# Moving the attention value products later in the output projections, and turning four score blocks on VectorE instead of TensorE

## The chip, the cores and the metric

The kernel runs on one core of one Trainium2 chip. The metric is the device time of one execution in microseconds (us), median over repeated runs; lower is better.

## The reference

One inference step of a two-layer decoder for two groups that share all weights: a prompt of 256 positions and 8 sample sequences of one position each, 264 columns in all. The width is 1024.

- Layer 0: norm, one input projection (q, k, v, bu, bv), block-sparse attention with 8 heads of 64 (half A of the mix) beside a gated mixer on bu and bv (half B), one output projection, residual.
- Layer 1: the same frame with stick-breaking attention (half A) and a pooling mixer (half B).
- Each layer then has a norm and a gated feed-forward part (2816 wide, causal convolution of width 3 on the gate), residual. A last norm ends it.

The output projection multiplies `concat([a, b_out])` by a 1024 x 1024 matrix. All of it is float32. Outputs are the two results, the new keys and values, the normalised bv rows of the samples, and pooling and convolution states.

## The kernel before, in words

**Products.** Activations lie as 8 tiles of 128 rows by 264 columns. Every weight matrix is cut into blocks of 128 x 128; a phase (`in0`, `out0`, `ff0`, `dn0`, and the same for layer 1) is a list of blocks (output tile m, input tile k), made in `_phases` (L62 to L78), and the host packs the weights in this order. A block costs three matmuls, since weight and activation are each split into a high and a low part of the faster float32 form (`wh`, `wl` and `..._h`, `..._l`). Eight blocks make a weight tile; `split` (L312) has ScalarE write `wh` (L322) and VectorE `wl` (L338) some tiles ahead: three as a rule, fewer where the tables `NEAR` and `LOOK` (L306, L307) say so. `split` also calls `raw` (L297), which loads the float32 weights, 1 MB for two tiles, into one of three buffers, up to two loads ahead.

**Order.** `run` (L365) goes through a phase block by block. TensorE runs in program order. A hook `blk(b, f)` calls f after b blocks of the phase, so its TensorE work stands between blocks, and its other instructions are ranked by that place. All transfers made with `late` (L284) go to SyncE's queue (SP) in program order, so that one that waits holds up those behind it. `behind(i, j)` only puts i after j on its engine.

**Output phases.** `out0` and `out1` are 64 blocks each. Before, four output tiles run side by side: first k = 4 to 7 (half B, the tiles `catB`) for m = 0 to 3, then k = 0 and 1 (half A, `catA`) for m = 0 to 3, then k = 2 and 3, tile by tile, then m = 4 to 7 one after the other. Each open output tile holds a PSUM bank: there are four of the pool `mm`, and four of the pool `at` that serve the small products; blocks listed in `spare` (L363) take one of `at`.

**The value products.** After 8 blocks of `out0` stand the sample products `pv` (L556), the value products `s_av` (L986, `pav`, two heads each), and `sm_out` (L1031, `po`), which together write `catA`. For them the score blocks p of each head must be turned, queries by keys to keys by queries:

- The first 256 columns of all heads go by VectorE's 32 x 32 transposes (`Turn.squares`, L605, tiles `turn0a`, `turn0b`), a write to DRAM (`write`, L610) and four reads back with the squares in their places (`read`, L614). The values take the same way (`turnv`, `v_squares`, L973), in eight reads.
- The last 128 columns of each head ("own") go by TensorE: `s_own` (L965) transposes four heads into PSUM, and ScalarE copies them out (`pT_own`). It is called for heads 0 to 3 after block 123 and for heads 4 to 7 after block 140 of `in0`.

Layer 1 turns its own blocks by VectorE's squares and DRAM (`own_squares`, `own_write`, `own_read`, L1290 to L1309). There the value products stand after 11 blocks of `out1`.

**Other work near it.** The gated mixer ends with `gm_gate` (L1106) and `gm_mul` (L1115), which write `catB`; tile 3 of it is made in `out0` after block 1. The residual input X is loaded after block 2 (`late_x`, L1140), and CSTATE, a state of the convolution, ahead of `out0`; `conv_prep` (L642) works on it.

Of the kernel before, what the change touches and what calls it, by code (L numbers as in the profile page):

```python
# [9 lines left out]
F32 = mybir.dt.float32  # L10
# [8 lines left out]
P = 128  # L19
D = 1024  # L20
KD = D // P
SEQ = 256
# [17 lines left out]
MMB = 4  # L40
KQ, MQ = 5, 6
WARM = 15

# [18 lines left out]
def _phases():  # L62
    k8 = list(range(KD))
    in0 = [(n, t) for n in ("bv", "q", "k", "v", "bu") for t in range(4)]
    q0 = [(m, k) for k in range(KQ) for m in in0[:MQ]] + [(m, k) for m in in0[:MQ] for k in range(KQ, KD)]
    in1 = [(n, t) for n in ("u", "q", "k", "v") for t in range(4)]
    m8 = [("o", t) for t in range(8)]
    kb = [4, 5, 6, 7, 0, 1, 2, 3]
    ff = [(n, j) for j in range(NF) for n in ("g", "u")]
    kf = list(range(NF))  # L70
    ph = []
    for l, ins in enumerate((in0, in1)):
        ph.append((f"in{l}", _split_order(ins, k8, 4) if l else q0 + [(m, k) for m in in0[MQ:] for k in k8]))
        ph.append((f"out{l}", [(m, k) for k in kb[:6] for m in m8[:4]] + [(m, k) for m in m8[:4] for k in kb[6:]] + [(m, k) for m in m8[4:] for k in kb]))
        ph.append((f"ff{l}", _split_order(ff, k8, 4)))
        two = [(m, k) for ks in (kf[:-2], kf[-2:]) for m in m8[:2] for k in ks]
        ph.append((f"dn{l}", two + [(m, k) for m in m8[2:] for k in (kf[2:] + kf[:2] if m[1] % 2 else kf)]))
    return ph  # L78
# [130 lines left out]
def tile_decoder_step(ctx: ExitStack, tc: tile.TileContext, a):  # L209
# [32 lines left out]
    def f4(name, shape=(P, 4, T), dt=F32):  # L242
        return up.tile(list(shape), dt, tag="u", name=name)
# [40 lines left out]
    def late(dst, src, queue=nc.sync):  # L284
        return tc.keep_in_program_order(queue.dma_start(dst, src))
# [19 lines left out]

    LOOK = {19: 1, 21: 2, 105: 2, 106: 2, 107: 2, 108: 1, 109: 1, 110: 0, 111: 2}  # L306
    NEAR = (3, 5, 10, 12, 15, 16, 17, 18)  # L307
# [4 lines left out]
    def split(t):  # L312
        if t == 2:
            raw(7)
        for tt in range(len(splits), min(t + (2 if t in NEAR else LOOK.get(t, 3)), NT - 1) + 1):
# [23 lines left out]
            if tt == 109:  # L339
                behind(i, turned["own", 0])  # L340
            if tt == 6:
                behind(i, summed)
# [19 lines left out]

    spare = (4, 5, 48)  # L363

# [204 lines left out]
    def sample_av_of(st, pz, vtiles, gr, name):  # L569
        return lambda: sample_av(st, pz, vtiles, gr, name)  # L570
# [25 lines left out]
    def flat(z):  # L596
        return z.rearrange({4: "p j x y -> p (j x y)", 5: "p j x y z -> p (j x y z)"}[len(z.shape)])

    class Turn:
# [13 lines left out]

        def read(self, parts=1, queue=nc.sync):  # L614
            self.dst = f4(f"{self.name}_turned", self.shape)
            far = self.far.rearrange("(i p) (j e x) -> p j i e x", i=4, j=4, e=parts)
            for j in range(4):
                to = flat(self.dst)[32 * j:32 * j + 32].rearrange("p (e i x) -> p i e x", i=4, e=parts)
                for e in range(parts):
                    late(to[:, :, e], far[:, j, :, e], queue)  # L620

# [342 lines left out]

    def s_own(n):  # L965
        pt = (mmb, at)[n](f"pt0_own{n}")
        for i in range(4):
            pe.transpose(pt[:, i * P:(i + 1) * P], st0.pop(("p", 4 * n + i))[:, SEQ:384], ident)
        if n == 0:
            st0["own"] = f4("pT0_own", (P, 8, P))  # L970
        turned["t", 3 + n] = s.activation(st0["own"][:, 4 * n:4 * n + 4, :], pt.rearrange("p (i q) -> p i q", q=P), AF.Copy)

    def v_squares(ts):  # L973
        if not turnv:
            turnv.append(Turn("turnv", (4, 2, 32, 4)))
        for t in ts:
            turned["vsq", t] = turnv[0].squares(t, v4[:, t, :], turnv[0].src[:, :, t // 2, :, t % 2::2].rearrange("p j b c -> p c j b"))
            behind(turned["vsq", t], turned["p", 7] if t > 1 else turned["v", 3])

    def v_of(c, h):  # L980
        t = h // 2
        return flat(turnv[0].dst).rearrange("p (e f x) -> p e f x", e=2, x=4)[:, t // 2, HD * (h % 2):HD * (h % 2) + HD, 2 * c + t % 2]

    turn0, turnv = [], []

    def s_av(t):  # L986
        if t == 0:
            catA.extend(mv("catA0"))
        pav = at(f"pav0_{t}")
        for h in (2 * t, 2 * t + 1):  # L990
            av(pav, v_of, turn0[h // 4].of(h % 4), st0["own"][:, h, :], h)
        turned["cat", t] = s.activation(catA[0][:, t, :SEQ], pav[:, :SEQ], AF.Copy)
        v.tensor_tensor(catA[1][:, t, :SEQ], pav[:, :SEQ], catA[0][:, t, :SEQ].bitcast(F32), ALU.subtract)
# [131 lines left out]
    def gm_bu(t):  # L1125
        turned["gelu", t] = s.activation(bu4[:, t, :], bu4[:, t, :], AF.Gelu_apprx_tanh)
        if t == 2:
            behind(turned["gelu", t], turned["sgu", 3])

# [10 lines left out]
    def late_x(m):  # L1140
        late(X[:, m:m + 2, :], a["x"].rearrange("p (m t) -> p m t", t=T)[:, m:m + 2, :])

# [31 lines left out]
    blk(143, sm_tr)  # L1174
    blk(156, lambda: late(a["bvn"], st0["bvn"]))
    for t in range(4):
# [4 lines left out]
    for t in range(3):  # L1181
        blk((138, 145, 153)[t], gm_bu, t)
# [12 lines left out]
    for t in range(4):  # L1195
        blk(8, s_av, t)
    blk(8, sm_out)
    blk(44, lnexp)


    late(CSTATE, a["cstate"].rearrange("p (l i j s) -> p l i j s", l=2, i=2, j=NF))
    for l in range(2):
        conv_prep(l)

# [79 lines left out]
    def z_squares(n):  # L1284
        for i in range(4):
            j = turned["w", 2 * n + 1] = turn1[n].squares(i, st1["w", 4 * n + i])
            if n:
                behind(j, turned["v", 0])

    def own_squares(n):  # L1290
        if n == 0:
            st1["own"] = f4("own1_squares", (P, 2, 4, 4, 32))
        for i in range(4):
            j = v.transpose(st1["own"][:, n, :, i, :], st1.pop(("w", 4 * n + i))[:, SEQ:384].rearrange("p (j b) -> p j b", j=4))
# [5 lines left out]
    def own_write(n):  # L1300
        st1["far", n] = drp.tile([P, 512], F32, tag=f"own1_{n}", name=f"own1_far{n}")
        late(st1["far", n], st1["own"][:, n].rearrange("p j i b -> p (j i b)"))

    def own_read(n):
        if n == 0:
            st1["turned"] = f4("own1_turned", (P, 2, 4, 4, 32))
        far = st1["far", n].rearrange("(a p) (j x) -> p j a x", a=4, j=4)
        for j in range(4):
            late(st1["turned"][32 * j:32 * j + 32, n].rearrange("p a i b -> p a (i b)"), far[:, j])  # L1309

    def z_av(t):
        if t == 0:
            catA.extend(mv("catA1"))
        pav = at(f"pav1_{t}")
        for h in (2 * t, 2 * t + 1):
            av(pav, lambda c, h: vt[:, c, h * HD:(h + 1) * HD], turn1[h // 4].of(h % 4), st1["turned"][:, h // 4, :, h % 4, :], h)
        halves(catA[0][:, t, :SEQ], catA[1][:, t, :SEQ], pav[:, :SEQ])
# [96 lines left out]
    blk(103, turn1[0].write)  # L1414
    blk(104, own_write, 0)
    blk(105, raw, 60)
    blk(105, z_squares, 1)
    blk(112, turn1[0].read)
    blk(112, own_read, 0)
    blk(119, lambda: turn1[1].write())  # L1420
# [10 lines left out]
    blk(2, own_squares, 1)  # L1431
    blk(2, own_write, 1)
    blk(2, own_read, 1)
    for t in (2, 3):
# [8 lines left out]
    for n, z in (("k1", k4), ("v1", v4)):  # L1443
        for i in (0, 2):
            blk(12, late, a[n][:, i:i + 2], z[:, i:i + 2])

# [75 lines left out]
```

## Time and profile before

| | |
|---|---|
| median of 3 runs | 576.15 us (576.0 to 576.34) |
| the profiled execution | 576.39 us |
| its span, first to last instruction | 574.6 us |
| TensorE busy | 569.6 us, 99% of the span |
| VectorE, ScalarE, GpSimd busy | 428.4, 341.8, 113.1 us |
| TensorE's share of the chain that ended last | 97% |
| mean granted TensorE clock | 0.999 |

"The chain that ended last" goes back from the last instruction, at each step to what released it or to the instruction before it on its engine. Work on other engines costs time only where it makes something on this chain wait.

### The profile page before, as it was taken

How to read it: one execution, taken by the hardware profiler on the slowest of the kernel's cores; microseconds unless marked ns; L12 is line 12 of the kernel's file. 1: busy time of each engine (PE TensorE's matmuls, PEld its weight loads, DVE VectorE, ACT ScalarE, POOL GpSimd, SP SyncE). 2: the span in 40 equal slices, each digit the busy share in tenths (PEclk: the TensorE clock that was granted, in tenths of full speed). 3: DMA queues.
4: the chain of work that ended last, by engine and by line, in shares of the span. 5: the costliest groups of instructions: out<-in, count | busy, mean ns of one | idle time of the engine just before them, and what ended most of it. 6: DMA issues, size and time to landing. Idle time of an engine off the chain costs nothing.

```text
span 574.6 us, 12309 instructions
## 1 busy us (share of the span) xinstructions
PE 569.6 (99%) x4865; PEld 555.9 (97%) x4865; DVE 428.4 (75%) x766; ACT 341.8 (59%) x606; POOL 113.1 (20%) x111
## 2 busy tenths in 40 slices
PE   9999999999999999999999999999999999999997
PEld 7998979999999999999999897999999999999996
DVE  6999978797777777865659887788777777775541
ACT  7847857765656555654454675667555565665442
POOL 1110113223232232210120011222222323211010
PEclk9999999999999999999999999999999999999999
DMA  8999889454545545795567697845455454555502
GB/s 322 361 386 362 315 266 384 161 211 148 201 165 178 189 159 209 271 407 210 185 233 266 237 332 197 305 155 204 165 168 200 155 211 149 194 208 200 213 1 76
DMA packets 33451, 128.69 MB, mean 224 GB/s; under 512 B 3954, under 2 KB 8946, under 8 KB 22002
## 3 DMA queue, kind: packets, MB, share of 16 engines
q1 hardware_dynamic: 32816, 127.39, 61.4%
q8 instruction: 38, 0.62, 0.4%
q10 hardware_dynamic: 578, 0.52, 0.3%
q14 instruction: 19, 0.16, 0.1%
HBM read 120.80 MB, written 7.10 MB: 223 GB/s over the span
## 4 chain that ended last, share of the span: by engine, by line
PE 97%; issue 2%; DMA 0%; ACT 0%; POOL 0%; DVE 0%; POOLq 0%; ACTq 0%
PE mm L221 90%; PE sc L221 1%; PE pv_l L221 1%; PE pav L221 1%; PE Z L221 1%; PE S L221 1%; DMA xw<-in_xw 0%; PE pf L221 0%; PE pm L221 0%; PE po_l L224 0%; PE vtp_sgu L224 0%; PE vtp_v L224 0%; PE pt_own L224 0%; POOL acc_fin L481 0%; PE ns_n L221 0%
## 5 line engine op out<-in xcount | busy, mean ns | idle before, releaser
L338 DVE TENSOR_TENSOR wl<-raw,wh 128x1024 fp32r<-128x1024 f32 x178 | 219.5, 1237 | 55.2 <-ACT wh L322 54.8
L322 ACT ACTIVATE wh<-raw 128x1024 fp32r<-128x1024 f32 x178 | 187.3, 1055 | 80.1 <-PE mm L221 68.4
L221 PE MATMUL mm<-xg_f_h,wl 128*128 128x264 f32 x704 | 197.5, 280 | 0.0
L221 PE MATMUL mm<-xg_f_h,wh 128*128 128x264 f32 x704 | 196.9, 280 | 0.0
L221 PE MATMUL mm<-xg_f_l,wh 128*128 128x264 f32 x704 | 196.8, 280 | 0.0
L221 PEld LDWEIGHTS mm<-xg_f_l,wh 128*128 128x128 f32 x704 | 131.9, 187 | 0.0
L221 PEld LDWEIGHTS mm<-xg_f_h,wl 128*128 128x128 f32 x704 | 131.8, 187 | 0.0
L221 PEld LDWEIGHTS mm<-xg_f_h,wh 128*128 128x128 f32 x704 | 131.8, 187 | 0.0
L684 POOL TENSOR_TENSOR wk<-wk 128x264 f32<-128x264 f32 x44 | 66.3, 1510 | 193.7 <-DVE wk L683 170.9
L221 PE MATMUL mm<-a_h,wl 128*128 128x264 f32 x330 | 92.6, 281 | 0.0
L221 PE MATMUL mm<-a_h,wh 128*128 128x264 f32 x330 | 92.3, 280 | 0.0
L221 PE MATMUL mm<-a_l,wh 128*128 128x264 f32 x330 | 92.3, 280 | 0.0
L221 PEld LDWEIGHTS mm<-a_l,wh 128*128 128x128 f32 x330 | 61.8, 187 | 0.0
L221 PEld LDWEIGHTS mm<-a_h,wh 128*128 128x128 f32 x330 | 61.8, 187 | 0.0
L221 PEld LDWEIGHTS mm<-a_h,wl 128*128 128x128 f32 x330 | 61.8, 187 | 0.0
L509 ACT ACTIVATE a_h<-wk 128x264 fp32r<-128x264 f32 x42 | 17.8, 423 | 70.2 <-POOL wk L684 70.2
L510 DVE TENSOR_TENSOR a_l<-wk,a_h 128x264 fp32r<-128x264 f32 x42 | 18.4, 438 | 40.0 <-ACT a_h L509 40.0
L221 PE MATMUL mm<-xg_h,wl 128*128 128x264 f32 x160 | 42.4, 288 | 0.0
L221 PE MATMUL mm<-xg_h,wh 128*128 128x264 f32 x160 | 42.1, 284 | 0.2 <-ACT wh L824 0.2
L221 PE MATMUL mm<-xg_l,wh 128*128 128x264 f32 x160 | 41.5, 281 | 0.0
L221 PE MATMUL mm<-xg_n_h,wl 128*128 128x264 f32 x128 | 36.5, 285 | 0.0
L221 PE MATMUL mm<-xg_n_h,wh 128*128 128x264 f32 x128 | 35.8, 280 | 0.0
(291 smaller groups left out, 931.4 us busy)
## 6 DMA issues: line engine op xcount, KB each, us to landing
raw<-in_w SPq DMA_DIRECT2D x89, 1024.0 KB, 4.8
K<-in_kt SPq DMA_DIRECT2D x32, 256.0 KB, 6.9
V<-in_vp SPq DMA_DIRECT2D x32, 256.0 KB, 6.4
raw<-in_w SPq DMA_DIRECT2D x3, 512.0 KB, 6.3
xw<-in_xw SPq DMA_DIRECT2D x3, 388.0 KB, 5.8
X<-in_x SPq DMA_DIRECT2D x4, 264.0 KB, 9.8
out_y<-y SPq DMA_DIRECT2D x3, 256.0 KB, 2.2
out_k<-k SPq DMA_DIRECT2D x1, 528.0 KB, 9.6
```

The source lines that it names most:

```text
L221: return self.keep(nc.tensor.matmul(*x, **k))
L322: i = s.activation(h, src, AF.Copy)
L338: i = turned["wl", tt] = v.tensor_tensor(l, src, h.bitcast(F32), ALU.subtract)
L509: s.activation(h, src, AF.Copy)
L510: return v.tensor_tensor(l, src, h.bitcast(F32), ALU.subtract)
L684: g.tensor_tensor(A, A, C, ALU.mult)
```

## The change

- In `out0` and `out1` five output tiles run side by side; the fifth takes a bank of the pool `at`. Half B now covers 20 blocks.
- Layer 0's value products stand after 16 blocks of `out0` (before 8), those of layer 1 after 14 of `out1` (before 11).
- Layer 0's own blocks of heads 4 to 7 go by VectorE's squares and DRAM, in a class `OwnTurn` that layer 1 now uses too. They are turned in `out0` after block 5, behind `wl` of tile 21, written and read back on SP.
- The values are stored in another order (8 elements between neighbours instead of 4), which takes four reads instead of eight; their last two squares stand behind `wl` of tile 19.
- X is loaded from ScalarE's queue; CSTATE and the bvn output move behind the own blocks' transfers, the k0 and v0 outputs to block 24; two gelus move; at tile 20 only one tile is converted ahead.

```diff
-        ph.append((f"out{l}", [(m, k) for k in kb[:6] for m in m8[:4]] + [(m, k) for m in m8[:4] for k in kb[6:]] + [(m, k) for m in m8[4:] for k in kb]))
+        ph.append((f"out{l}", [(m, k) for k in kb[:6] for m in m8[:MO]] + [(m, k) for m in m8[:MO] for k in kb[6:]] + [(m, k) for m in m8[MO:] for k in kb]))
...
-    LOOK = {19: 1, 21: 2, 105: 2, 106: 2, 107: 2, 108: 1, 109: 1, 110: 0, 111: 2}
+    LOOK = {19: 1, 20: 1, 21: 2, 105: 2, 106: 2, 107: 2, 108: 1, 109: 1, 110: 0, 111: 2}
...
+            if tt == 22:
+                behind(i, turned["own0"])
...
-    spare = (4, 5, 48)
+    spare = (4, 5, 48, 164, 884)
...
+    class OwnTurn:
...
+        def square(self, n, i, w):
+            return v.transpose(self.all[:, n, :, i, :], w[:, SEQ:384].rearrange("p (j b) -> p j b", j=4))
+
+        def write(self, n):
+            self.far[n] = drp.tile([P, 512], F32, tag=f"{self.name}{n}", name=f"{self.name}_far{n}")
+            late(self.far[n], self.all[:, n].rearrange("p j i b -> p (j i b)"))
+
+        def read(self, n):
+            far = self.far[n].rearrange("(a p) (j x) -> p j a x", a=4, j=4)
+            for j in range(4):
+                late(self.turned[32 * j:32 * j + 32, n].rearrange("p a i b -> p a (i b)"), far[:, j])
...
+    def s_own_squares():
+        own0.append(OwnTurn("own0", 1))
+        for i in range(4):
+            turned["own0"] = own0[0].square(0, i, st0.pop(("p", 4 + i)))
+            behind(turned["own0"], turned["wl", 21])
+        own0[0].write(0)
+        own0[0].read(0)
...
-            behind(turned["vsq", t], turned["p", 7] if t > 1 else turned["v", 3])
+            behind(turned["vsq", t], turned["wl", 19] if t > 1 else turned["v", 3])
...
-            av(pav, v_of, turn0[h // 4].of(h % 4), st0["own"][:, h, :], h)
+            av(pav, v_of, turn0[h // 4].of(h % 4), own0[0].of(0, h % 4) if h > 3 else st0["own"][:, h, :], h)
...
-        late(X[:, m:m + 2, :], a["x"].rearrange("p (m t) -> p m t", t=T)[:, m:m + 2, :])
+        behind(late(X[:, m:m + 2, :], a["x"].rearrange("p (m t) -> p m t", t=T)[:, m:m + 2, :], s), turned["gelu", 3])
...
-    for f in (lambda: turn0[1].write(), lambda: turnv[0].write(), lambda: turn0[0].read()):
+    for f in (lambda: turn0[1].write(), lambda: turn0[0].read(), lambda: turnv[0].write(), lambda: turn0[1].read(), lambda: turnv[0].read()):
         blk(143, f)
-    blk(143, lambda: turn0[1].read())
-    blk(143, lambda: turnv[0].read(2))
...
-    blk(123, s_own, 0)
+    blk(123, s_own)
...
-    blk(136, v_squares, (2, 3))
-    blk(140, s_own, 1)
+    blk(137, v_squares, (2, 3))
...
+    blk(1, raw, 15)
...
-    blk(5, late, a["k0"], k4)
-    blk(5, late, a["v0"], v4)
+    blk(5, s_own_squares)
+    blk(6, late, a["bvn"], st0["bvn"])
+    blk(6, late, CSTATE, a["cstate"].rearrange("p (l i j s) -> p l i j s", l=2, i=2, j=NF))
+    for l in range(2):
+        blk(6, conv_prep, l)
+    blk(24, late, a["k0"], k4)
+    blk(24, late, a["v0"], v4)
...
-        blk(8, sample_av_of(st0, PZ, vtiles, i, "l0"))
+        blk(16, sample_av_of(st0, PZ, vtiles, i, "l0"))
     for t in range(4):
-        blk(8, s_av, t)
-    blk(8, sm_out)
+        blk(16, s_av, t)
+    blk(16, sm_out)
...
-        blk(11, sample_av_of(st1, PZ, vtiles, i, "l1"))
+        blk(14, sample_av_of(st1, PZ, vtiles, i, "l1"))
     for t in range(4):
-        blk(11, z_av, t)
-    blk(11, zs_out)
+        blk(14, z_av, t)
+    blk(14, zs_out)
```

## Rows read from the trace of the kernel before

**Rows 1.** The page, busy time: engine, us, share of the span, instructions.
```profile
PE 569.6 (99%) x4865; PEld 555.9 (97%) x4865; DVE 428.4 (75%) x766; ACT 341.8 (59%) x606; POOL 113.1 (20%) x111
```
**Rows 2.** The chain that ended last: start us, us, what, instructions.
```profile
63.78 0.44 PE pt_own L224 x4
...
77.56 3.57 PE pv_l L221 x32
81.13 2.97 PE pav L221 x31
...
84.68 25.78 PE mm L221 x216
...
356.42 2.80 PE pav L221 x32
```
**Rows 3.** All waits of TensorE over the whole span: total us, times, longest.
```profile
PE warm L221 <- PEq L1488: 0.8, 1, 0.8
PE mm L221 <- ACT wh L824: 0.2, 1, 0.2
```
**Rows 4.** Timeline of SP's queue in layer 0: start us, us, issues.
```profile
74.02 4.03 SPq L285 DMA_DIRECT2D turnv_turned<-turnv_far  x8
78.47 0.36 SPq L285 DMA_DIRECT2D raw<-in_w  x1
...
80.34 2.07 SPq L285 DMA_DIRECT2D X<-in_x  x4
```
**Rows 5.** Transfers issued from 66 to 79.69 us: KB each, median us to landing.
```profile
raw<-in_w SPq DMA_DIRECT2D x1, 1024.0 KB, 5.2
...
CSTATE<-in_cstate SPq DMA_DIRECT2D x1, 352.0 KB, 5.3
out_bvn<-bvn SPq DMA_DIRECT2D x1, 16.0 KB, 4.9
```
**Rows 6.** Transfers over the whole span, own blocks of layer 1, same columns.
```profile
own_far<-own_squares SPq DMA_DIRECT2D x2, 256.0 KB, 2.8
...
own_turned<-own_far SPq DMA_DIRECT2D x8, 64.0 KB, 2.2
```
**Rows 7.** Timelines of SP's and ScalarE's queues in layer 1, the turned blocks.
```profile
349.98 0.34 SPq L285 DMA_DIRECT2D own_far<-own_squares  x1
352.85 1.74 SPq L285 DMA_DIRECT2D own_turned<-own_far  x4
...
350.08 2.48 ACTq L285 DMA_DIRECT2D turn1b_turned<-turn1b_far  x4
```
**Rows 8.** Timeline of all engines from 76 to 92 us, value products and their end.
```profile
82.93 0.49 PE L221 MATMUL pav<-pT_own,turnv_turned 128*64 128x128 f32 x4
...
85.89 0.23 DVE L1038 TENSOR_TENSOR catA_l<-osam,catA_h 128x32 fp32r<-128x32 f32 x1 [0.30 <-ACT catA_h L1037]
```
**Rows 9.** Timeline of VectorE around the start of `out0`.
```profile
75.07 3.49 DVE L338 TENSOR_TENSOR wl<-raw,wh 128x1024 fp32r<-128x1024 f32 x3
78.47 0.43 DVE L1118 TENSOR_TENSOR catB_l<-bu,catB_h 128x264 fp32r<-128x264 f32 x1
...
79.74 0.44 DVE L1118 TENSOR_TENSOR catB_l<-bu,catB_h 128x264 fp32r<-128x264 f32 x1 [0.49 <-ACT catB_h L1117]
```
**Rows 10.** Timeline of ScalarE around the start of `out0`.
```profile
73.15 2.94 ACT L322 ACTIVATE wh<-raw 128x1024 fp32r<-128x1024 f32 x3
...
76.31 0.41 ACT L1126 ACTIVATE bu<-bu 128x264 f32<-128x264 f32 x1
```
**Rows 11.** Layer 1's own squares on VectorE: duration ns min/median/max, starts, shape.
```profile
L1294 DVE STREAM_TRANSPOSE own_squares<-w x8: 268/269/304, 335.5 to 349.7; 128x128 f32<-128x128 f32 x8
```
**Rows 12.** Windows: us, busy of PE, PEld, DVE, ACT, POOL, granted clock, DMA share, GB/s.
```profile
84.00:88.00 4.00, 4.00 (x35) 3.98 (x34) 2.70 (x8) 1.90 (x4) 3.16 (x6) 1.00 1.01 397
570.00:573.00 3.00, 0.59 (x5) 0.35 (x5) 0.89 (x3) 0.95 (x3) 0.32 (x1) 1.00 0.95 357
573.00:574.60 1.60, 0.00 (x0) 0.00 (x0) 0.00 (x0) 0.00 (x0) 0.00 (x0) 0.65 0.02 7
```

More of the change, by code (lines that the diff above doesn't have):

```diff
@@ L41 @@
 KQ, MQ = 5, 6
+MO = 5
 WARM = 15
@@ L612, in write, with read @@
             late(self.far, flat(self.src))
-        def read(self, parts=1, queue=nc.sync):
+        def read(self, queue=nc.sync):
             self.dst = f4(f"{self.name}_turned", self.shape)
-            far = self.far.rearrange("(i p) (j e x) -> p j i e x", i=4, j=4, e=parts)
+            far = self.far.rearrange("(i p) (j x) -> p j i x", i=4, j=4)
             for j in range(4):
-                to = flat(self.dst)[32 * j:32 * j + 32].rearrange("p (e i x) -> p i e x", i=4, e=parts)
-                for e in range(parts):
-                    late(to[:, :, e], far[:, j, :, e], queue)
+                late(flat(self.dst)[32 * j:32 * j + 32].rearrange("p (i x) -> p i x", i=4), far[:, j], queue)
         def of(self, i):
@@ L963, in s_squares, with s_own @@
             behind(turned["p", h], turned["bvn"])
-    def s_own(n):
-        pt = (mmb, at)[n](f"pt0_own{n}")
+    def s_own():
+        pt = mmb("pt0_own")
         for i in range(4):
[L968 to L971, printed above, removed]
+            pe.transpose(pt[:, i * P:(i + 1) * P], st0.pop(("p", i))[:, SEQ:384], ident)
+        st0["own"] = f4("pT0_own", (P, 4, P))
+        turned["t", 3] = s.activation(st0["own"], pt.rearrange("p (i q) -> p i q", q=P), AF.Copy)
@@ new lines, in tile_decoder_step, with __init__, of @@
+    class OwnTurn:
+        def __init__(self, name, n):
+            self.name, self.far = name, {}
+            self.all = f4(f"{name}_squares", (P, n, 4, 4, 32))
+            self.turned = f4(f"{name}_turned", (P, n, 4, 4, 32))
+        def square(self, n, i, w):
[7 more added lines that the diff above has]
+                late(self.turned[32 * j:32 * j + 32, n].rearrange("p a i b -> p a (i b)"), far[:, j])
+        def of(self, n, i):
+            return self.turned[:, n, :, i, :]
@@ L973, in v_squares @@
+    own0 = []
+    def s_own_squares():
[5 more added lines that the diff above has]
+        own0[0].read(0)
     def v_squares(ts):
         if not turnv:
-            turnv.append(Turn("turnv", (4, 2, 32, 4)))
+            turnv.append(Turn("turnv", (4, 32, 8)))
         for t in ts:
-            turned["vsq", t] = turnv[0].squares(t, v4[:, t, :], turnv[0].src[:, :, t // 2, :, t % 2::2].rearrange("p j b c -> p c j b"))
@@ L978, in v_squares @@
-            behind(turned["vsq", t], turned["p", 7] if t > 1 else turned["v", 3])
+            turned["vsq", t] = turnv[0].squares(t, v4[:, t, :], turnv[0].src[:, :, :, t::4].rearrange("p j b c -> p c j b"))
+            behind(turned["vsq", t], turned["wl", 19] if t > 1 else turned["v", 3])
     def v_of(c, h):
-        t = h // 2
-        return flat(turnv[0].dst).rearrange("p (e f x) -> p e f x", e=2, x=4)[:, t // 2, HD * (h % 2):HD * (h % 2) + HD, 2 * c + t % 2]
+        return turnv[0].dst.rearrange("p i b x -> p (i b) x")[:, HD * (h % 2):HD * (h % 2) + HD, 4 * c + h // 2]
@@ L1126, in gm_bu @@
         turned["gelu", t] = s.activation(bu4[:, t, :], bu4[:, t, :], AF.Gelu_apprx_tanh)
-        if t == 2:
-            behind(turned["gelu", t], turned["sgu", 3])
+        if t in (1, 2):
+            behind(turned["gelu", t], turned["sgu", 2 * t - 1])
     hk = Hooks()
@@ L1174, in tile_decoder_step @@
     blk(143, sm_tr)
-    blk(156, lambda: late(a["bvn"], st0["bvn"]))
     for t in range(4):
@@ L1181, in tile_decoder_step @@
     for t in range(3):
-        blk((138, 145, 153)[t], gm_bu, t)
+        blk((138, 150, 153)[t], gm_bu, t)
         blk((154, 154, 157)[t], gm_mul, t)
@@ L1189, in tile_decoder_step @@
     blk(1, gm_mul, 3)
-    blk(5, late, a["k0"], k4)
-    blk(5, late, a["v0"], v4)
+    blk(5, s_own_squares)
[5 more added lines that the diff above has]
+    blk(24, late, a["v0"], v4)
     blk(24, late, a["cs"], CSTATE[:, :, 1])
     for i in range(2):
-        blk(8, sample_av_of(st0, PZ, vtiles, i, "l0"))
+        blk(16, sample_av_of(st0, PZ, vtiles, i, "l0"))
     for t in range(4):
-        blk(8, s_av, t)
-    blk(8, sm_out)
+        blk(16, s_av, t)
+    blk(16, sm_out)
     blk(44, lnexp)
-    late(CSTATE, a["cstate"].rearrange("p (l i j s) -> p l i j s", l=2, i=2, j=NF))
-    for l in range(2):
-        conv_prep(l)
     xg, nrm, evac = residual(vec("f0"), "f0")
@@ L1288, in z_squares @@
                 behind(j, turned["v", 0])
+    own1 = []
     def own_squares(n):
         if n == 0:
-            st1["own"] = f4("own1_squares", (P, 2, 4, 4, 32))
+            own1.append(OwnTurn("own1", 2))
         for i in range(4):
-            j = v.transpose(st1["own"][:, n, :, i, :], st1.pop(("w", 4 * n + i))[:, SEQ:384].rearrange("p (j b) -> p j b", j=4))
+            j = own1[0].square(n, i, st1.pop(("w", 4 * n + i)))
             behind(j, turned["wl", 110 if n else 108])
@@ L1298, in own_squares @@
             turned["own", n] = j
[L1300 to L1309, printed above, removed]
     def z_av(t):
@@ L1315, in z_av @@
         for h in (2 * t, 2 * t + 1):
-            av(pav, lambda c, h: vt[:, c, h * HD:(h + 1) * HD], turn1[h // 4].of(h % 4), st1["turned"][:, h // 4, :, h % 4, :], h)
+            av(pav, lambda c, h: vt[:, c, h * HD:(h + 1) * HD], turn1[h // 4].of(h % 4), own1[0].of(h // 4, h % 4), h)
         halves(catA[0][:, t, :SEQ], catA[1][:, t, :SEQ], pav[:, :SEQ])
@@ L1414, in tile_decoder_step @@
     blk(103, turn1[0].write)
-    blk(104, own_write, 0)
+    blk(104, lambda: own1[0].write(0))
     blk(105, raw, 60)
@@ L1418, in tile_decoder_step @@
     blk(112, turn1[0].read)
-    blk(112, own_read, 0)
+    blk(112, lambda: own1[0].read(0))
     blk(119, lambda: turn1[1].write())
@@ L1431, in tile_decoder_step @@
     blk(2, own_squares, 1)
-    blk(2, own_write, 1)
-    blk(2, own_read, 1)
+    blk(2, lambda: own1[0].write(1))
+    blk(2, lambda: own1[0].read(1))
     for t in (2, 3):
@@ L1438, in tile_decoder_step @@
     for i in range(2):
-        blk(11, sample_av_of(st1, PZ, vtiles, i, "l1"))
+        blk(14, sample_av_of(st1, PZ, vtiles, i, "l1"))
     for t in range(4):
-        blk(11, z_av, t)
-    blk(11, zs_out)
-    for n, z in (("k1", k4), ("v1", v4)):
-        for i in (0, 2):
-            blk(12, late, a[n][:, i:i + 2], z[:, i:i + 2])
+        blk(14, z_av, t)
+    blk(14, zs_out)
+    for i in (0, 2):
+        blk(15, late, a["k1"][:, i:i + 2], k4[:, i:i + 2])
+    blk(15, late, a["v1"], v4)
     xg, nrm, evac = residual(vec("f1"), "f1")
```

## The prediction

> **What bounds the kernel now.** I read the page's busy times first: TensorE is busy for 569.6 of 574.6 us, and no other engine for more than 75% [rows 1]. That alone could hide waits, so the waits come next: TensorE's own list has two, 1.0 us in all, both at the start [rows 3]. The chain of waits then shows what fills the time: TensorE from one piece to the next, with nothing between. A long stretch behind the value products of layer 0 gives its pace, 25.78 us for 216 matmuls, 0.119 us each and 0.358 us a block of three [rows 2]. So TensorE is the bound. A change gains only what it takes off TensorE, and loses whatever it makes TensorE wait for; all that VectorE, ScalarE and the queues win costs or gives nothing by itself.
>
> **What is removed.** The four transposes of `s_own` for heads 4 to 7 stand on the chain with 0.44 us [rows 2]: **-0.44 us**. Their copy out of PSUM is off the chain. All else on TensorE stays: `pv`, `pav`, `po` and 64 blocks per output phase, in another order. The largest gain that I can find is therefore 0.44 us, plus at most the 0.17 us by which layer 0's `pav` is longer than layer 1's (2.97 against 2.80) [rows 2]. These 0.17 us are the most I would ascribe to the values' spacing of four elements, and no trace shows a spacing of eight: bounds -0.17 and, if it doubles, +0.17; I take 0, since one value in a place of its own is read as before.
>
> About 0.2% is what a measurement here can tell from no change: 1.15 us. A saving of 0.44 us is under half of that, so "faster" by more would need a cause that I don't see.
>
> **What is added, by the time it is needed.** The own blocks of heads 4 to 7 now come back through DRAM. TensorE reads them first in head 4's second product. Today this is at 82.93 [rows 8]; it moves by -0.44 and by eight blocks of 0.358, +2.86, to **85.35**. The way there:
>
> - VectorE: four squares, 0.27 us each [rows 11], 1.1 us behind `wl` 21. Today three `wl` start at 75.07 [rows 9], of which the new look-ahead leaves one there, so the squares are through by about 77.5. VectorE has the time for it, as the two other `wl` (2.3 us of the 3.49) go behind them, and their tiles are first used after the value products.
> - SP's queue: the write is behind a 1 MB weight load (`raw` 15). The new line `blk(1, raw, 15)` does nothing: look-ahead for tile 20 calls that load at block 144 of `in0`, and it shows behind the turned reads, at 78.47 [rows 4]. With four reads of the values instead of eight, whose issue took 4.03 us, I put it 2.0 us earlier, at 76.4. It landed 5.2 us after its issue; the 16 KB of bvn, issued just behind, took 4.9, and CSTATE, 352 KB, 5.3 [rows 5]. So a small transfer lands behind the large one ahead of it on its queue: weights at 81.6. CSTATE, issued some 0.8 us after the weights (two issues of about 0.4), landed 0.9 us after them; 256 KB should take 0.7: write landed at 82.3.
> - The reads wait on SP for that. In layer 1 they took 1.74 us to issue, and each lands 2.2 us after its issue [rows 6, 7]: 1.3 + 2.2 = 3.5 us, so 85.8.
>
> That is 0.45 us late with nothing else in flight. If SP gets to the weights 1.2 us sooner, at 75.2 (the values' write now goes out between the two sets of reads, so the wait for its landing may be hidden), it is 0.75 us early. With no weights ahead, as in layer 1 (write 349.98, reads from 352.85) [rows 7], it would be 2.8 + 3.5 = 6.3 us from 77.5, 83.8.
>
> **The second addition is X.** Its four loads leave SP, where they stood behind all of this, for ScalarE's queue, behind the last gelu. That gelu is at 76.31 today, behind three `wh` of 2.94 us [rows 10]; two of them go, so the loads are issued from about 75 on, for some 2.07 us [rows 4], beside the weights and own blocks. Four times 264 KB are 1.08 MB; at the 397 GB/s of a full DMA stretch [rows 12] that is 2.7 us of all engines. No trace of before has two queues with large transfers at once. Bounds: none of X ahead of the own blocks, 0; all of it, +2.7. The nearest rows are layer 1's reads of `turn1b` on ScalarE's queue, beside which an own write kept its 2.8 us [rows 6, 7]; they are small, but they are all there is, so I take a value nearer the low end: 0.6. The wait of TensorE is then 0.45 + 0.6 = **+1.0 us**, its ends 0 and 3.2.
>
> [...]
>
> Behind the waiting reads stand on SP: bvn, CSTATE and the next weights. The weights are needed at block 48 of `out0`, 74.3 + 48 x 0.358 + 7.1 for the products between (77.56 to 84.68) = 98.6 [rows 2]; issued by 86 and landed some 6 us later they are in time. CSTATE serves the feed-forward part. Nobody waits.
>
> **Edits that I cost at nothing.** `catB` tiles 2 and 3 are now needed at blocks 10 and 15, at 77.8 and 79.6 (start of `out0` at 77.56 - 0.44 - 2.86 = 74.26). Today they end at 78.90 and 80.18, behind three `wl` [rows 9]. With two of these moved off they are some 2.3 us sooner, 76.6 and 77.9; without that cover, tile 2 would cost 1.1 us. Layer 1: own reads land by 354.2 + 2.2 = 356.4, head 4 needs them at 357.8 (1.4 us into `pav`) [rows 2, 6, 7]; three more blocks only widen this. The output tiles' evacuations move later and closer together, with the conversions three tiles ahead as cover. The end of `catA` in layer 0 has four blocks now instead of eight: 1.43 us, and from the end of `po` (84.68) to the last low half it takes 1.44 (86.12) [rows 2, 8], with 0.12 to spare as the low half comes second: 0, at worst +0.3. One PSUM bank fewer for the small products is 0, at worst +0.2 a layer.
>
> **Sum.** -0.44 + 1.0 = +0.56: 576.39 becomes 576.95 for the profiled execution, whose span is 1.8 us less, and it stood 0.24 above the median. On the median: **576.7 us**.
>
> **Rivals.**
> - *The return is in time.* The weights leave by 75.2 and X costs nothing. For it: bounds above, 0.75 us early. Against: three terms must all be short. -0.44: 575.7.
> - *X and the weights go first (the other side).* TensorE stands in `pav` before head 4's own product until SP's reads have landed. It decides once X delays the write by over 1.15 us, so that the wait passes 1.6. By the bytes [rows 12] X costs up to 2.7: wait 3.2, 578.9. Priced at a wait of 2.6: +2.2, 578.3. For it: such loads fill all engines at 84 to 88 [rows 12], and X is issued ahead of the weights. Against: the own write of layer 1 [rows 6, 7]. [...]
> - *Banks and the end of `catA`.* In time on the reads, but two output phases each wait some tenths: +0.3 to +0.7, less 0.44: 576.2.
> [...]
>
> **How the numbers follow.** Forecast (wait 0.3 to 1.6): 0.32. In time: 0.25. X first: 0.30. Banks: 0.07. Clock: 0.03. Something unseen that gains over 0.2%: 0.03. Forecast, in time and banks lie within 1.15 us of 576.15: 0.64 same. Slower: 0.30 + 0.03 = 0.33. Faster: 0.03. The range goes from 575.4 (in time, `pav` shorter, a little spread) to 578.9 (all of X ahead); outside are the clock, the unseen gain and the edges of the two large cases, under 0.2. The likeliest case alone: 576.0 to 577.3.
>
> **What would show it.** In the chain, four `pt_own` less at 63 us, and no other TensorE group shorter. In the waits, a wait of `pav` on the transfer of own0's read, of about 1 us; none means "in time". In the transfers, own0's write landing just after the weights, and X landing beside them: if the write takes over 7 us, X went first. A wait of the first `catA` block on VectorE, or of `pav` on the copies, means banks. Wrong altogether would be a TensorE wait anywhere else, or a granted clock below 1.00 before 570 us.

## The result and the profile after

| | before | after |
|---|---|---|
| median | 576.2 us (5 runs, 576.0 to 576.52) | **581.89 us** (5 runs, 581.3 to 582.48) |
| ratio to before | | 1.0097, 95% interval 1.0082 to 1.0111 |
| the profiled execution | 576.39 us | 581.44 us |
| its span | 574.6 us | 579.7 us |

The change makes the kernel 5.7 us slower; the forecast was +0.5, and the range ended at 578.9. The page of the kernel after, busy time and one queue (packets, MB, share of 16 engines):

```profile
PE 571.7 (99%) x4861; PEld 557.5 (96%) x4861; DVE 429.3 (74%) x770; ACT 340.4 (59%) x605; POOL 116.4 (20%) x111
...
q10 hardware_dynamic: 1154, 1.61, 1.0%
```

The work is as foreseen: four matmuls less and four transposes of VectorE more [rows 1]. q10 is ScalarE's queue, which now also carries X (1.61 MB, before 0.52). The chain that ended last, from 69 to 91 us:

```profile
69.49 5.69 DMA turnv_far<-turnv_squares
...
75.27 0.78 DVE catB_l L1149 x2
...
77.46 6.30 PE mm L222 x39
83.75 3.57 PE pv_l L222 x32
87.33 3.43 PE pav L222 x28
```

Before, TensorE alone made up this stretch [rows 2]; now it starts on a transfer, and catB's low halves. The 39 matmuls take 6.30 us and not 39 x 0.119 = 4.64, and `pav` takes 3.43 and not 2.97. `pt_own` is gone at 63 us. TensorE's waits over the whole span:

```profile
PE mm L222 <- DVE catB_l L1149: 2.1, 1, 2.1
PE warm L222 <- PEq L1509: 0.8, 1, 0.8
PE mm L222 <- DVE bu L926: 0.3, 1, 0.3
```

Nothing of own0 and nothing of layer 1 is in this list. The windows tell the rest (TensorE's busy time and matmuls, granted clock, DMA share, GB/s):

```profile
72.00:74.00 2.00, 1.69 (x15) 1.00 0.99 295
74.00:76.00 2.00, 0.24 (x2) 1.00 0.37 102
76.00:78.00 2.00, 1.65 (x10) 0.68 0.68 205
78.00:80.00 2.00, 2.00 (x11) 0.50 1.02 299
80.00:82.00 2.00, 2.00 (x18) 0.97 0.97 378
```

TensorE stands from 73.7 to 75.8 us, does a little, and then has the clock at 0.50 until 80.1: a matmul every 0.22 us where it was 0.12.

**The sum.** The first norm of layer 0 starts at 20.10 us (before 20.54), the norm at its end at 302.69 (before 298.25); between the two the change adds 4.88 us. Four transposes: -0.44. The waits, counted from one matmul's start to the next one's: 2.9 (the list gives 2.4, since a matmul is shown 0.28 us long and the next starts after 0.12). The low clock: 6.30 - 4.64 = 1.66. `pav`: 0.46. A wait of the feed-forward's norm: 0.3. Together 4.9. Layer 1 adds nothing: its `pav` takes 2.80 us in both [rows 2]. Another 0.6 us lies behind the last matmul of the profiled execution; no run tells why.

The low clock belongs to this execution and not to the loss. A fall to half for 3.4 us takes 0.003 off the mean clock of a run of 580 us. Of the five runs two have a mean of 0.996 and 0.997 (581.44 and 581.3 us); the three with 0.998 or 1.000 took 581.92, 581.89 and 582.48 us and were no faster.

**Where the waits come from.** SyncE's queue, ScalarE with its queue, and VectorE, in this order:

```profile
69.49 0.38 SPq L286 DMA_DIRECT2D turnv_far<-turnv_squares  x1
69.97 3.06 SPq L286 DMA_DIRECT2D turn0b_turned<-turn0b_far  x4
75.24 1.73 SPq L286 DMA_DIRECT2D turnv_turned<-turnv_far  x4
77.08 0.36 SPq L286 DMA_DIRECT2D raw<-in_w  x1
79.71 0.34 SPq L286 DMA_DIRECT2D own_far<-own_squares  x1
83.55 1.74 SPq L286 DMA_DIRECT2D own_turned<-own_far  x4
...
88.38 0.86 SPq L286 DMA_DIRECT2D raw<-in_w  x2
```

```profile
82.31 5.79 ACTq L286 DMA_DIRECT2D X<-in_x  x4
88.20 0.60 ACT L570 ACTIVATE msk<-pv_l 128x512 f32<-128x512 f32 x1 [5.48 <-DMA own_turned<-own_far]
```

```profile
75.27 0.78 DVE L1149 TENSOR_TENSOR catB_l<-bu,catB_h 128x264 fp32r<-128x264 f32 x2 [2.64 <-DMA turnv_far<-turnv_squares]
...
79.60 2.33 DVE L339 TENSOR_TENSOR wl<-raw,wh 128x1024 fp32r<-128x1024 f32 x2
81.83 0.43 DVE L1147 TENSOR_TENSOR bu<-bu,bv 128x264 f32<-128x264 f32 x1
```

Before, in the same three timelines:

```profile
68.32 0.33 SPq L285 DMA_DIRECT2D turnv_far<-turnv_squares  x1
72.94 0.78 DVE L1118 TENSOR_TENSOR catB_l<-bu,catB_h 128x264 fp32r<-128x264 f32 x2
81.27 0.60 ACT L567 ACTIVATE msk<-pv_l 128x512 f32<-128x512 f32 x1 [1.57 <-PE pv_l L221]
```

Three things are to be seen. `catB_l` of the first tile stood 2.64 us on VectorE until the *write* of the values' squares had landed, 5.69 us after its issue. Ahead of `msk`, which empties `pv`'s PSUM bank, ScalarE did no work for 5.48 us: it was issuing X's four loads. And the product of catB's last tile (81.83) stood behind own squares and two `wl`.

### The profile page after: what moved, and what is told of

It reads as the page before. It is cut to its first block, busy times and chain, and to the rows that moved or that the text cites. A ratio compares the mean times of both kernels' runs of the same rounds, so it can differ in the third digit from the quotient of the medians.

```text
span 579.7 us, 12304 instructions
## 1 busy us (share of the span) xinstructions
PE 571.7 (99%) x4861; PEld 557.5 (96%) x4861; DVE 429.3 (74%) x770; ACT 340.4 (59%) x605; POOL 116.4 (20%) x111
## 3 DMA queue, kind: packets, MB, share of 16 engines
q10 hardware_dynamic: 1154, 1.61, 1.0%
## 4 chain that ended last, share of the span: by engine, by line
PE 91%; DVE 4%; issue 2%; DMA 1%; ACT 0%; SPq 0%; POOL 0%; POOLq 0%; DVEq 0%; ACTq 0%
PE mm L222 85%; DVE wl L339 2%; PE sc L222 1%; PE pv_l L222 1%; PE pav L222 1%; DMA turnv_far<-turnv_squares 1%; DVE xg_f_l L464 1%; PE warm L222 1%; PE Z L222 1%; PE S L222 1%; DVE X L712 0%; SPq L286 0%; PE pm L222 0%; ACT wh L323 0%; PE vtp_v L225 0%
```

## The experiments

Times stand beside runs of the kernel before on the same chip (medians 576.1 to 576.3 us).

**E1: the write of the values first, as before.** In the kernel after, at block 143:

```diff
-turn0[1].write, turn0[0].read, turnv.write, turn0[1].read, turnv.read
+turn0[1].write, turnv.write, turn0[0].read, turn0[1].read, turnv.read
```

> The changed kernel with one line turned back: the values' write to DRAM goes out ahead of the four reads of turn0a, as before. Theory S (a tile's place in SBUF): catB_l takes the place of the values' squares, so VectorE may not write it before that write has landed; the write landed 5.7 us after its issue because it was queued behind four reads, VectorE stood 2.6 us, TensorE 2.2 us at the start of out0, and its clock fell. S expects the write landed by 71.5 us, no wait of catB_l, no fall of the clock, and 575.7 to 577.5 us. Rival Q (the queues: X on ScalarE's queue and the own blocks' return are what costs): the order makes no difference, 580 to 582 us.

Measured: 582.65 us, ratio 1.0103 (1.0087 to 1.012). Missed. The write lands at 73.09 and TensorE starts `out0` without the long wait, but the time is not better. ScalarE with its queue, then TensorE's largest wait:

```profile
80.22 8.56 ACTq L286 DMA_DIRECT2D X<-in_x  x4
88.88 0.60 ACT L570 ACTIVATE msk<-pv_l 128x512 f32<-128x512 f32 x1 [8.25 <-DMA own_turned<-own_far]
```

```profile
PE pav L222 <- ACT msk L570: 2.6, 1, 2.6
```

With the first wait gone, TensorE is earlier and meets the second: `pav` of heads 4 and 5 needs the bank that `msk` has to empty. In the profiled execution the 1.25 us of catB's last tile and 3.4 us at half the clock behind the new wait come on top (583.65 us; one of the four runs, with a mean clock of 1.000, took 581.68).

**E2: the late write alone, in the kernel before.**

```diff
-turn0[1].write, turnv.write, turn0[0].read
+turn0[1].write, turn0[0].read, turnv.write
```

> The kernel before with that order alone changed: four reads of turn0a ahead of the values' write. S: the same wait of VectorE at catB_l for the write, 2 to 3 us, TensorE waiting at the start of out0, 578 to 581.5 us. Q: nothing of X or own blocks is changed, 576 to 576.5 us.

Measured: 578.22 us, ratio 1.003 (1.0019 to 1.0041). As expected. VectorE:

```profile
75.56 0.78 DVE L1118 TENSOR_TENSOR catB_l<-bu,catB_h 128x264 fp32r<-128x264 f32 x2 [2.65 <-DMA turnv_far<-turnv_squares]
```

The same wait of VectorE in the kernel before; alone it costs 2 us by the medians. The profiled execution is the slowest of eight (580.17 us) and the only one whose mean clock, 0.995, shows a fall.

**E3: the values' squares in X's memory**, so that catB does not take over their place; the order of the transfers stays that of the change.

```diff
-turnv.append(Turn("turnv", (4, 32, 8)))
+turnv.append(Turn("turnv", (4, 32, 8), X.rearrange("p m t -> p (m t)")[:, :1024].rearrange("p (j b x) -> p j b x", j=4, b=32)))
```

> The changed kernel, order as changed, but the values' squares are put into the memory of X (loaded only later), so that catB_l finds another place. The write lands as late as in the changed kernel. S: no wait of catB_l for that write, no fall of the clock, 575.7 to 578 us. A theory in which the late write itself costs (the values come back too late) or Q: 580 to 582 us.

Measured: 582.36 us, ratio 1.0124 (1.0081 to 1.0166). VectorE:

```profile
72.27 1.01 DVE L1149 TENSOR_TENSOR catB_l<-bu,catB_h 128x264 fp32r<-128x264 f32 x2
```

`catB_l` no longer waits, although the write lands only at 74.86; in the kernel after it starts 0.09 us behind the landing (75.18). So the wait is for the place: catB's low half is given the memory of the squares, and gets it when their write to DRAM has landed. The time, 4 us above theory S's range, stays where it was for E1's reason (ScalarE held for 8.05 us, `pav` 2.2 us on `msk`).

**E4: the out phases alone**, in the kernel before: five tiles, the two spare banks, the products 8 and 3 blocks later.

```diff
+MO = 5
...
-    spare = (4, 5, 48)
+    spare = (4, 5, 48, 164, 884)
...
-        blk(8, s_av, t)
+        blk(16, s_av, t)
```

> The kernel before with five output tiles side by side and the value products after 16 and 14 blocks, nothing else. S: no transposes removed and no write delayed, so 576.2 us and up to 1 us more for catB tile 2, which is needed sooner behind three wl: 576.0 to 577.3 us. Rival P (the fifth tile's bank and the four blocks behind the sample products cost in both layers): 577.5 to 580 us, with waits of pav on the copies.

Measured: 577.68 us, ratio 1.0024 (1.0014 to 1.0034). The time, 1.5 us above before, lies in the rival's range and 0.4 us above that of S; but the rival's sign, a wait of `pav` on the copies, is not there. 0.7 us of it are a wait on catB's third tile, behind three `wl` on VectorE; the rest stays open here.

**E5 to E7: the waits taken away one after another.** E5: the kernel after with X on SyncE again, behind own0's transfers. E6: also the write first. E7: also catB ahead of the weights on VectorE:

```diff
-        behind(late(X[:, m:m + 2, :], ..., s), turned["gelu", 3])
+        late(X[:, m:m + 2, :], ...)
...
-        blk(2, late_x, m)
+        blk(7, late_x, m)
...
             if tt == 22:
                 behind(i, turned["own0"])
+                behind(i, turned["gate", 3])
```

> The changed kernel with X loaded by SyncE's queue again, behind own0's transfers and CSTATE; the order of the transfers at block 143 stays that of the change. Theory S (two waits in series: first the place of catB_l, held until the late write of turnv has landed; then ScalarE, which stands 5.8 us or more in issuing X, because two of X's four loads wait for the completion of raw 15 and of own0's first read; each wait hides the other): the first wait of some 2.2 us and the low clock behind it stay, and ScalarE is no longer held, so msk follows pv within 0.5 us. In the changed kernel the second wait showed only 0.16 us of its own, so the time falls by little: 580.5 to 582 us. Theory O (one cause, X on ScalarE's queue, and the rest follows from it): 576 to 577.5 us.

> The same with the write of turnv put ahead of the reads of turn0a again, as in the kernel before: both suspected waits taken away. Theory S: no wait of TensorE on a copy of catB's first tile over 0.6 us and none of pav's on msk; what is left is the product of catB's last tile, which stands on VectorE behind own0's squares and two wl (1.25 us of wait in the run with the write alone moved): 576.5 to 578.5 us, 3 to 5 us below the change, although each of the two edits alone gives under 1 us. Rival B (TensorE waits for own0's read-back, or for banks, as soon as it comes to the late blocks in time): 579 us or more, with a wait of pav that ends on own0's last read.

> The same again, and wl 22 and 23 put behind the last copy of catB on VectorE. Theory S: the wait on catB's last tile (1.25 us) goes too; what remains of the change is four transposes of TensorE less (0.44 us) and the own squares: 575.5 to 576.5 us, the same as before or a little faster. Rival W (wl 22 is needed at once, so that the wait moves to the weights of the next tile): no better than the run without this edit, with a wait of TensorE on wl in its place.

Measured: 582.58, 582.43 and 581.74 us (ratios 1.0112, 1.0106, 1.0102, each within 0.0017). In E5 `msk` follows `pv` at once and the time stays, as expected, 0.6 above the range. E6 and E7 are misses by 4 and 5 us: in E7 three known waits are gone, and nothing is gained. E6 came as its rival B had it, with `pav` waiting for own0's read-back. TensorE's waits in E7:

```profile
PE pav L222 <- DMA own_turned<-own_far: 2.2, 1, 2.2
PE ns_f L222 <- DVE nl_f L514: 0.9, 1, 0.9
...
PE mm L222 <- DVE bu L927: 0.5, 1, 0.5
```

In E6 (0.8 us by its list) and here the wait of the forecast appears. In E7 own0's write is issued at 78.33, 1 us behind `raw` 15, and its first read, which waits for it at the head of SyncE's queue, at 85.28: 6.9 us. CSTATE, X and `raw` 16 stand behind those reads; `raw` 16 is issued at 89.97 (before, 79.87), and the norm of the feed-forward pays.

**E8: X on ScalarE's queue alone**, in the kernel before.

```diff
-        late(X[:, m:m + 2, :], ...)
+        behind(late(X[:, m:m + 2, :], ..., s), turned["gelu", 3])
```

> The kernel before with one edit: X is loaded by ScalarE's queue, behind the last gelu, as the change does; no own0 and the old order of transfers. Theory S (what holds ScalarE is not X's own loads but that they take the completion semaphores of transfers still under way): here the semaphores in turn are those of the reads of turn0b and turnv, under way since 74 to 78 us, so ScalarE is held under 3 us and pav waits under 1 us: 576 to 577.3 us. Rival X (four loads on ScalarE's queue cost by themselves): 577.5 to 579 us, with msk over 4 us behind pv.

Measured: 584.78 us, ratio 1.0146 (1.013 to 1.0163): worse than the whole change, and more than either theory gave. ScalarE with its queue, TensorE's waits, and the windows (us; TensorE, its weight loads, VectorE, ScalarE, GpSimd; clock, DMA share, GB/s):

```profile
83.58 5.58 ACTq L285 DMA_DIRECT2D X<-in_x  x4
89.20 0.60 ACT L567 ACTIVATE msk<-pv_l 128x512 f32<-128x512 f32 x1 [9.59 <-DMA raw<-in_w]
```

```profile
PE pav L221 <- ACT msk L567: 6.5, 1, 6.5
```

```profile
84.00:88.00 4.00, 0.00 (x0) 0.00 (x0) 0.00 (x0) 0.00 (x0) 2.95 (x6) 1.00 0.97 299
88.00:92.00 4.00, 2.15 (x11) 1.46 (x12) 1.17 (x4) 1.81 (x5) 0.00 (x0) 0.52 1.06 432
```

The mechanism is theory S's, with other holders than I named. In the traces of the kernels before and after, each with 232 transfers on its two queues, eight completion semaphores have 29 transfers each. In each of the two, 196 transfers follow one on the same semaphore whose landing the trace has: none went out before that landing, the nearest 0.02 us behind it. Here X's first load goes out at 83.58, 5.29 us after the issue of `raw` 15, which took 5.2 to land before [rows 5]; the fourth at 88.82, `raw` 16 having landed at 88.80. In the kernel after, the fourth goes out at 87.77, own0's first read, on the same semaphore, having landed at 87.74. ScalarE does no work in between, 9.59 us in all with the 4.0 us ahead of the first load, and `msk` stands behind.

**E9: `raw` 15 and X behind own0's transfers**, otherwise E7. **E10: the out phases alone**, with the change's look-ahead and E7's order on VectorE.

```diff
 E9
-                raw(c)
+                if c != 15 or own0:
+                    raw(c)
     blk(5, s_own_squares)
+    blk(5, raw, 15)
+    for m in range(0, KD, 2):
+        blk(5, late_x, m)
```

```diff
 E10, against E4
-    LOOK = {19: 1, 21: 2, ...}
+    LOOK = {19: 1, 20: 1, 21: 2, ...}
+            if tt == 22:
+                behind(i, turned["gate", 3])
```

> The version with X by SyncE, turnv's write first and catB's last copy ahead of wl 22, and now raw 15 (one 1 MB load of weights) and X issued behind own0's write and reads, not ahead of them. Theory Q (own0's write stands in the queue behind raw 15: 6.9 us with raw 15 issued 1 us ahead of it, though such a write takes 2.6 to 3.5 us elsewhere; its reads wait for it at the head of SyncE's queue and hold up raw 16 and X behind them, which is the 1.2 us at the norm of the feed-forward): the write lands within 4 us, its reads 3 us later, the wait of pav on them falls from 2.5 us to under 0.6, the wait at the norm to under 0.4: 576 to 577.5 us. Rival R (the write is slow of itself, or the read-back cannot be hidden where it stands, whatever is ahead of it): the wait of pav stays over 1.5 us and the time over 579.

> The kernel before with the parts of the change that concern the out phases (five tiles side by side, the two spare banks, products 8 and 3 blocks later), the weights' look-ahead of the change, and wl 22 behind the last copy of catB: heads 4 to 7 by TensorE, X and all transfers as before. Theory: the 0.72 us wait on the copy of catB's third tile goes, because one or two wl less stand ahead of it on VectorE, and what is left of the phases' price is about 0.5 us: 576.2 to 577.0 us, so the phases by themselves neither help nor hurt and the 5.7 us all come from own0 and the transfers moved for it. Rival: the phases cost over 1 us whatever the order on VectorE: 577.3 us or more.

Measured: E9 579.87 us, ratio 1.0063 (1.0049 to 1.0077); E10 578.69, ratio 1.0047 (1.0033 to 1.006). Half of theory Q holds: own0's write lands in 3.4 us and `pav` takes 3.47 us, 0.5 more than before. But both kernels have new waits of TensorE behind 95 us, E9 2.5 us by its list and E10 1.9 (E9's profiled execution is its slowest, 1.8 us above the median). E10 has neither own0 nor moved transfers, and was to be 576.2 to 577.0; it lies in its rival's range. Its SyncE queue and its ScalarE show the cause:

```profile
83.59 1.16 SPq L286 DMA_DIRECT2D raw<-in_w  x2
```

```profile
93.99 2.01 ACT L323 ACTIVATE wh<-raw 128x1024 fp32r<-128x1024 f32 x2 [3.90 <-DMA raw<-in_w]
```

`raw` 16 is asked for when tile 22 comes into the look-ahead. `LOOK` 20:1 puts that 8 blocks later, behind X and the k output.

**E11: E9 with own0's reads on ScalarE's queue and `raw` 16 right behind `raw` 15. E12: E10 with `raw` 16 at its old place.**

```diff
 E11
-        own0[0].read(0)
+        own0[0].read(0, s)
+    blk(5, raw, 16)
```

```diff
 E12
+    blk(1, raw, 16)
     for m in range(0, KD, 2):
         blk(2, late_x, m)
```

> The version with raw 15 behind own0's write, and now own0's four reads on ScalarE's queue behind the last catB_h, so that SyncE does not stand for them, and raw 16 asked for right behind raw 15. (The change's look-ahead of the weights, LOOK 20:1, also puts off the request of raw 16: it was issued at 79.9 us before, at 88.4 in the change.) Theory V (the weights' loads from 80 to 100 us run on engines that are full, so each load issued later comes up as a wait on wh or wl or as wl ahead of nl_f near 95 to 114 us): raw 16 is issued by 82 us, the waits of 1.2, 0.7 and 1.2 us of TensorE at 110 to 114 us go down to 0.3 in all, own0's reads cost under 0.5: 576.3 to 577.8 us. Rival W (not the loads but VectorE's order, wl 22 behind catB's last copy with five tiles evacuated together, makes wl late): the waits at 110 to 114 us stay over 2 us in all and the time over 578.5.

> The out phases alone with wl 22 behind catB's last copy, and raw 16 asked for at its old place (in the run without this, 578.69 us, ScalarE stood 3.9 us for raw 16, and TensorE 1.15 us at 95.6 us and 1.2 us at the norm). Theory V: both waits go to 0.3 us or less in all: 576.2 to 576.9 us. Rival W: they stay, 578 us or more.

Measured: E11 585.86 us, ratio 1.0158 (1.0144 to 1.0172); E12 576.94, ratio 1.0013 (1.0004 to 1.0023). E12 bears out theory V: TensorE's waits fall to 0.2 us, and the out phases cost 0.8 us (0.2 to 1.3 by the interval), so E10's rival falls. E11 missed its range by 8 us. The waits near 110 us go in it too (0.3 left), but ScalarE is held once more:

```profile
82.50 6.00 ACTq L286 DMA_DIRECT2D own_turned<-own_far  x4
88.60 0.60 ACT L572 ACTIVATE msk<-pv_l 128x512 f32<-128x512 f32 x1 [9.84 <-DMA own_turned<-own_far]
```

The first read, at 82.50, had to wait for own0's write (issued at 78.02). The fourth goes out at 88.19, `raw` 16, issued at 79.26, having landed at 88.17.

**E13: E9 with `raw` 16 ahead of X. E14: own0's squares 9 us earlier, right behind those of turn0b**, its transfers with theirs, and `raw` 15, `raw` 16 and X in the order of the kernel before.

```diff
 E14, against E7
-            behind(turned["own0"], turned["wl", 21])
+            behind(turned["own0"], turned["p", 7])
-    blk(5, s_own_squares)
+    blk(136, s_own_squares)
+    blk(1, raw, 16)
```

> The version with X by SyncE, turnv's write first, wl 22 behind catB's last copy and raw 15 behind own0's transfers (579.87 us), and now raw 16 right behind raw 15, ahead of X. Theory V (weights): raw 16 is issued near 85.3 us in place of 89.0, so the waits of 1.24, 0.69 and 1.20 us of TensorE at 110 to 114 us fall to under 1.5 in all; 0.62 at 75.4 us stays: 577.3 to 578.8 us, between the run with raw 16 late and the out phases alone. Rival F (own0 has no price of its own once raw 16 is early): 576.9 us or less.

> Own0's squares right behind those of turn0b on VectorE (near 68 us, 9 us earlier), its write ahead of turnv's, its reads behind turnv's, raw 15, raw 16 and X in the order of the kernel before. Theory D (VectorE is full from 65 to 76 us: TensorE already waits 0.62 us for a bank that bu's copy has to free): the four squares (1.0 us) delay everything behind them, so this wait and that on catB's first copy grow by up to 1 us in all, and nothing else waits: 576.8 to 578.0 us. Rival F (VectorE has 1 us to spare there): 576.0 to 576.7 us, 0.44 us of it TensorE's four transposes. Rival L (SyncE's four more reads put raw 15 and raw 16 back by 2 us, and the weights are late again): waits over 1 us in all at 90 to 114 us, 578 us or more.

Measured: E13 580.15 us, ratio 1.007 (1.0056 to 1.0083); E14 **577.87**, ratio 1.003 (1.0019 to 1.0041). E13 missed its range: `raw` 16 goes out at 84.95 (before, 79.87) and the wait of 1.24 us falls to 0.23, but the norm still waits (0.9 on `nl_f`, 0.5 on `nh_f`); why was not tried. E14's time lies in theory D's range, but that is luck: the two waits that D had growing are gone. TensorE's only wait behind the start is for `pf`, a product of the gated mixer that reads `vgt`, and `vgt` comes from ScalarE. VectorE's own squares, and these two:

```profile
66.77 0.85 DVE L982 STREAM_TRANSPOSE own_squares<-p 128x128 f32<-128x128 f32 x4
```

```profile
70.31 0.66 ACT L591 ACTIVATE vgt<-vtp_sgu 128x256 f32<-128x256 f32 x2 [2.47 <-DMA own_far<-own_squares]
```

```profile
70.80 1.13 PE L222 MATMUL pf<-sguc,vgt 128*128 128x128 f32 x8 [0.98 <-issue]
```

ScalarE stood 2.47 us until own0's *write* had landed at 70.21, 2.56 us after its issue, and made `vgt` 0.10 us later. `vgt` uses no value of own0, so this looks like the first wait again, at another place: `vgt` would be given the memory of own0's squares. A version with the squares elsewhere, as in E3, was not tried. Between layer 0's first norm and the norm at its end the profiled execution is 0.9 us slower than before: 1.1 for this wait, counted from start to start, -0.44 for the transposes, and 0.2 that show in no wait. Another 0.6 us lies behind the last matmul, as in the kernel after.

## Why the prediction was wrong

Both signs that the prediction gave for being wrong altogether were there: a wait of TensorE where none was expected, on `catB_l`, and, in two of the five runs, a clock below 1.00 ahead of 570 us.

- **"-0.44 us" for the transposes** was right. From the first norm to `vtp_sgu`, TensorE is 0.47 us faster.
- **The order of reads and values' write, costed at nothing, is the step that failed first.** I asked what the later write does to SyncE and wrote that "the wait for its landing may be hidden". I did not ask who else waits for it. VectorE does, for the memory (E2: 2.0 us by itself, E3: the wait goes with the memory). It took the write from 3.2 us to 5.69, with four reads ahead, to make it decide. In E14 the same question went unasked for own0's write.
- **"The second addition is X" was priced in the wrong unit.** I asked how many bytes go ahead of own0's and took 0.6 of at most 2.7 us. What counts is that issuing is work of ScalarE, in its order, and that an issue can stand for another transfer's landing: ScalarE did no work for 5.5 us in the kernel after and for 7.8 to 9.6 in E3, E1 and E8, with TensorE behind it through a PSUM bank. Alone this costs 8.7 us (E8). Nor did the loads go out from about 75: they stand behind catB's last high half in ScalarE's order, which came at 82.30. I listed what stands behind the waiting reads on SyncE, but not what stands behind the loads on ScalarE; `msk` would have been the first name there.
- **The wait for own0's read-back, +1.0 us (0 to 3.2)**, lay within its ends where the other waits were away: 2.5 us in E7, 1.1 in E6, 0.5 with the write ahead of the weights (E9). In the kernel after it does not show, since TensorE is by then 3 us late. Its terms were off: the squares are through at 79.7 and not 77.5, the reads at 89.0 and not 85.8.
- **The look-ahead (`LOOK` 20:1)** helped catB only in part: its last product stood at 81.83, behind own squares and two `wl`, where I had its copy done by 77.9. That it also asks for `raw` 16 later was priced by TensorE's need alone (block 48, 98.6). The engines that convert it wait first: in E10 it lands at 93.88, ScalarE stands 3.90 us for it, and on VectorE the evacuation that TensorE waits for at 95.6 stands behind its `wl`. In the kernel after this is covered by the other delays, in E10 it costs 1.8 us (578.69 against 576.94 in E12).
- **The clock**, a chance of 0.03 for a fall after a long wait, came true in two of the five runs, but costs nothing that the medians show: the runs without a fall were as slow. The wait ahead of the fall was that on `catB_l`, 2.2 us, not one on own0's reads; that its length brings the fall on is not shown (E7: 2.5 us, and the clock stayed at 1.00).
- **Layer 1, the spacing of the values, banks and catA's end at nothing** were right as far as the waits show: layer 1's `pav` takes 2.80 us as before, layer 0's 2.99 in E14 and 2.97 before, and no run waits on banks. The out phases as a whole cost 0.8 us (E12), of which 0.2 are a wait; the rest is open.

So the sign of the larger rival was right and its mechanism was not. The loss is a row of five waits, each of which hides the next: the place of `catB_l`, ScalarE's held issue, catB's last product on VectorE, own0's write behind the weights, `raw` 16. Taking away one, two or three (E1, E3, E5 to E7) changed the time by less than 1 us. With all five gone (E14) 4 us come back. What is left of own0's price is mostly a sixth wait, 1.1 us behind the landing of its own write, more than the 0.44 us of TensorE that it saves. No version beat the kernel before; it was not tried whether E14 does without that wait.

## What to carry to other kernels

Before a transfer is moved, list everything that its *landing* sets free: the data, the memory it reads from (here 2.64 us of VectorE's time), and the completion semaphore that a later transfer, on any queue, may have to wait for (9.59 us of ScalarE's in E8); then ask which engine takes that wait, and what stands behind it there. A transfer on a computing engine's queue stood here among that engine's instructions (the issue of X's four loads took ScalarE 5.58 us in E8): it belongs there only where nothing urgent follows. And if one undone edit gives nothing back, that does not clear it: undo it together with the next wait that shows, until the sum comes out.

## What the runs showed of the hardware

- Whether the clock falls is not settled by the kernel, nor by the length of one wait (counted from start to start). In the profiled executions it fell to half (0.50), for 3.4 us, after waits of 1.6 us (E2), 2.2 (after), 2.4 (E3) and 2.8 (E1), and for 6.8 us after one of 6.7 (E8) and after two of 3.5 and 2.0 (E11); with a wait of 1.8 us in E5 and of 2.5 in E7 it stayed at 1.00. But other runs of the same kernels differ: means of 0.995 in E5 and of 0.995 and 0.996 in E7, and 0.998 to 1.000 in three of five of the kernel after. What decides was not tried.
- A queue of its own did not make a small transfer quick: in E11 the last of own0's reads, 64 KB on ScalarE's queue, landed 3.43 us after its issue, beside loads of X on SyncE's. On SyncE's queue these reads took 2.0 us in the median in E7, 2.7 in E14 and 3.1 in E9, and 4.1 in the kernel after, with X on ScalarE's.
- Transfers of both queues were under way at once: in the kernel after X's third load, issued at 83.19 us on ScalarE's queue, landed at 87.56, and own0's four reads, issued from 83.55 to 84.87 on SyncE's, from 87.74 to 88.99. The first two loads of X had landed at 84.92 and 85.63. Nothing of X went ahead of own0's write, issued at 79.71: X went out from 82.31 on, and the first read, which waits for that write, at 83.55.
